# RWKV's block inverses: both chunks of a head in one product with the whole block-diagonal matrix

## The chip, the cores and the metric

The kernel runs on one core of one Trainium2 chip. Its time is the device time of one execution in microseconds (us). The core's engines are TensorE (PE in the profile, its loads of stationary operands PEld), VectorE (DVE), ScalarE (ACT), GpSimd (POOL) and SyncE (SP); each works through a queue of its own in order, and they meet at semaphores.

## The reference, cut to what matters

The program is three transformer layers over 512 tokens of 1024 features: an RWKV-7 time mix with a SwiGLU, a gated spatial mixer with a SwiGLU, and an attention layer with a feed-forward of 16384 single-neuron experts (PEER). All is float32. The change lies in the time mix, whose core is a recurrence over tokens, for each of 16 heads, with a 64x64 state S:

```
def step(S, inp):
    r_t, w_t, k_t, v_t, a_t, b_t = inp
    sa = jnp.einsum('bhij,bhj->bhi', S, a_t)
    S = (S * w_t[:, :, None, :] + sa[..., None] * b_t[:, :, None, :] + v_t[..., None] * k_t[:, :, None, :])
    y = jnp.einsum('bhij,bhj->bhi', S, r_t)
    return S, y
```

## The kernel before, in words

The recurrence is computed in chunks of 64 tokens. Inside a chunk the term `sa` of a token depends on those of the tokens before it, which makes a 64x64 unit triangular system for each head and chunk; its inverse, transposed, is the tile TT. A unit is 128 tokens (two chunks) by 8 heads, so there are 4 x 2 = 8 units. The rows of a tile are the 128 tokens, chunk 0 in partitions 0 to 63 and chunk 1 in 64 to 127.

A loop in `rwkv` (L607 to L618) staggers three stages of different units. For each k it writes out: the chain of unit k-3 (`wkv_chain`, which carries the state on), the solve of unit k-2 (`wkv_solve`), the preparation of unit k (`wkv_prep`), and the output step of unit k-3 (`wkv_post`, vector work).

- `wkv_prep` transposes its inputs on PE (L663), multiplies them (L678), copies the diagonal blocks into Ma on ACT (L681) and writes the masked products M on DVE (L682). The blocks go through DRAM (dl) into the tile L in which one 16x16 block has one partition; DVE inverts these small blocks (L704 to L719), and they return through DRAM to two tiles Nd and NdT in which they stand on the diagonal of each 64x64 block.
- `wkv_solve` multiplies the rest of the system with Nd (L740) and copies the result into Yd on ACT (L741), one copy for each chunk. Yd is 128 x 8 heads x 128: of a head's 128x128 matrix the two 64x64 blocks on the diagonal are written and the other two were set to zero at the start (`wkv_init`). Three products with Yd follow (L749), each with an addition of NdT on DVE (L750); the addition's result is the moving operand of the next product, and the third gives TT.
- `wkv_chain` uses TT (L780) between lines that multiply with M and the state (L773, L775, L785, L794, L795).

The work of all three stages is queued on PE together. The order in each engine's queue is made when the program is built, not by the order of the lines alone, so pieces of L749 stand between lines of the other stages. After the stage the program goes on with the output projection; its weights are split into two parts on ACT and DVE (L102, L103), and some of these splits stand among the last units' work.

A matmul takes a stationary operand, loaded first, and a moving one. In a product of L749 the stationary operand is one chunk's 64 columns of Yd (128 rows by 64 columns), the moving one is 64 columns of the current iterate, and the result goes to the 64 partitions of that chunk. A float32 matmul shows in the profile as two passes.

Of the kernel before, what the change touches and what calls it, by code (L numbers as in the profile page):

```python
# [40 lines left out]
class Kern:  # L41
# [689 lines left out]
    def wkv_solve(self, p2, Yd, u):  # L731

        nc = self.nc
        mm = nc.tensor.matmul
        Nd, NdT = u["N"]
        bk = self.bank("s")
        for c in range(2):
            r = slice(64 * c, 64 * c + 64)
            for e in range(8):
                mm(bk[r, e * 64:(e + 1) * 64], u["M"][r, c, e, r], Nd[r, e, :], start=True, stop=True)  # L740
            nc.scalar.copy(Yd[r, :, r], bk[r].rearrange("p (e n) -> p e n", e=8))  # L741
        cur = NdT
        for it in range(3):
            nxt = p2.tile([128, 8, 64], F32, name="TT" if it == 2 else "TTt", bufs=2)
            bk = self.bank("s")
            for e in range(8):
                for c in range(2):
                    r = slice(64 * c, 64 * c + 64)
                    mm(bk[r, e * 64:(e + 1) * 64], Yd[:, e, r], cur[:, e, :], start=True, stop=True)  # L749
            nc.vector.tensor_add(nxt, bk.rearrange("p (e n) -> p e n", e=8), NdT)  # L750
            cur = nxt
        u["TT"] = cur
# [929 lines left out]
```

## Time and profile before

| | |
|---|---|
| median of 3 runs | 3100.21 us (3096.3 to 3103.62) |
| the profiled execution | 3095.69 us, its span 3093.9 us |
| PE busy | 2951.7 us, 95% of the span, 16121 passes |
| PEld busy | 2483.1 us, 80% |
| DVE, ACT, POOL busy | 68%, 37%, 21% |
| granted clock of PE over the span | 0.971 of full speed |
| L749 in the trace | 768 passes between 333 and 490 us |

Busy shares are averages over stages of different kinds. Matmuls are pipelined, the next starts long before the last has ended, and the ends are modelled: the duration of a group is the time from its first start to its last end, and the distance between starts is what a pass costs its successors.

### The profile page before, as it was taken

The numbers are of one execution on the slowest core, as the hardware profiler recorded it, in microseconds if no ns is written. First come the engines' busy times: TensorE is split into PE (matmuls) and PEld (weight loads), VectorE is DVE, ScalarE is ACT, GpSimd is POOL, SyncE is SP. The second block draws the span as 40 slices with busy tenths as digits, with TensorE's granted clock in tenths as the row PEclk, the third lists the DMA queues.
The fourth block names the chain that finished last, engine by engine and source line by source line (L and its number), as shares of the span: only waits on it lengthen the run. The fifth ranks groups of instructions, "written<-read, shape, count | busy, mean of one in ns | idle before, by whom it ended". The sixth has DMA issues, their size and how long they took to land.

```text
span 3093.9 us, 43610 instructions
## 1 busy us (share of the span) xinstructions
PE 2951.7 (95%) x16121; PEld 2483.1 (80%) x16121; DVE 2091.1 (68%) x4694; ACT 1156.3 (37%) x1918; POOL 646.3 (21%) x593
## 2 busy tenths in 40 slices
PE   7977899999999999999999999989999999999998
PEld 6755787888888788888875888989999888787887
DVE  7663775533247666425776678999988477888787
ACT  5533433322223332223565433344433333333332
POOL 1023221000000000000000003345444434444453
PEclk9978999999999999999998999999999999999999
DMA  4235654222324267533220234678888889999996
GB/s 143 92 85 192 162 144 130 93 91 95 95 89 143 76 214 234 164 95 92 77 85 2 68 101 161 227 244 294 282 292 287 294 307 322 336 341 321 327 335 223
DMA packets 217553, 569.03 MB, mean 184 GB/s; under 512 B 64474, under 2 KB 80090, under 8 KB 217212
## 3 DMA queue, kind: packets, MB, share of 16 engines
q1 hardware_dynamic: 144508, 362.71, 35.8%
q0 software_dynamic: 64096, 200.89, 19.1%
q10 hardware_dynamic: 8736, 2.65, 0.4%
q8 instruction: 126, 2.06, 0.3%
q14 instruction: 87, 0.71, 0.1%
HBM read 504.24 MB, written 61.87 MB: 183 GB/s over the span
## 4 chain that ended last, share of the span: by engine, by line
PE 75%; DVE 12%; DMA 6%; issue 4%; ACT 2%; POOL 1%; POOLq 0%; SPq 0%; DVEq 0%; ACTq 0%
PE b L276 19%; PE b L124 15%; PE b L123 15%; PE b L122 15%; PE b L1470 3%; DMA gl<-ga 2%; DVE wlo L103 2%; DVE er L1304 1%; PE b L1161 1%; PE b L959 1%; DVE hr L1308 1%; DMA er<-in_pe_ur,eu 1%; PE b L1179 1%; DVE wk L1339 1%; PE b L678 1%
## 5 line engine op out<-in xcount | busy, mean ns | idle before, releaser
L102 ACT CAST whi<-wst 128x1024 fp32r<-128x1024 f32 (+2 forms) x491 | 510.7, 1041 | 1165.4 <-PE b L123 436.1
L103 DVE TENSOR_TENSOR wlo<-wst,whi 128x1024 fp32r<-128x1024 f32 (+2 forms) x466 | 563.3, 1210 | 442.5 <-ACT whi L102 426.2
L124 PE MATMUL b<-hTh,wlo 128*128 128x384 f32 (+2 forms) x1992 | 716.4, 360 | 13.7 <-DVE wlo L103 13.4
L122 PE MATMUL b<-hTh,whi 128*128 128x384 f32 (+2 forms) x1992 | 722.4, 363 | 2.5 <-ACT hTh L223 1.5
L123 PE MATMUL b<-hTl,whi 128*128 128x384 f32 (+2 forms) x1992 | 717.0, 360 | 2.2 <-DVE hTl L224 2.2
L124 PEld LDWEIGHTS b<-hTh,wlo 128*128 128x128 f32 x1992 | 377.7, 190 | 57.0 <-DVE wlo L103 18.4
L122 PEld LDWEIGHTS b<-hTh,whi 128*128 128x128 f32 x1992 | 379.2, 191 | 42.3 <-ACT hTh L223 2.2
L123 PEld LDWEIGHTS b<-hTl,whi 128*128 128x128 f32 x1992 | 378.4, 190 | 40.9 <-DVE hTl L224 3.0
L122 PE MATMUL b<-whi,ch 128*128 128x512 f32 x768 | 304.7, 397 | 5.4 <-ACT ch L102 5.4
L124 PE MATMUL b<-whi,cl 128*128 128x512 f32 x768 | 304.6, 397 | 1.2 <-DVE cl L103 1.2
L123 PE MATMUL b<-wlo,ch 128*128 128x512 f32 x768 | 304.5, 396 | 0.3 <-DVE wlo L103 0.3
L1292 POOL DMA_INDIRECT er<-in_pe_v,ev x128 | 196.0, 1531 | 241.1 <-DVE hr L1308 216.1
L1292 POOL DMA_INDIRECT er<-in_pe_ur,eu x128 | 171.6, 1340 | 90.1 <-DVE er L1304 58.5
L122 PEld LDWEIGHTS b<-whi,ch 128*128 128x128 f32 x768 | 144.8, 189 | 39.8 <-ACT ch L102 5.7
L124 PEld LDWEIGHTS b<-whi,cl 128*128 128x128 f32 x768 | 144.6, 188 | 36.8 <-DVE cl L103 2.0
L123 PEld LDWEIGHTS b<-wlo,ch 128*128 128x128 f32 x768 | 144.8, 189 | 34.9 <-DVE wlo L103 0.7
L1308 DVE SCALAR_TENSOR_TENSOR hr<-er,a,hr 128x1024 f32<-128x1024 f32 x127 | 164.4, 1294 | 0.1
L1304 DVE SCALAR_TENSOR_TENSOR er<-er,hr 128x1024 f32<-128x1024 f32 x128 | 156.3, 1225 | 8.5 <-DMA er<-in_pe_ur,eu 8.5
L1274 POOL DMA_DIRECT2D ga<-gl x112 | 64.8, 579 | 345.1 <-ACT gl L1269 332.0
L276 PE MATMUL b<-whi,hTh 128*128 128x512 f32 (+2 forms) x336 | 129.3, 386 | 0.8 <-ACT P L971 0.8
L276 PE MATMUL b<-whi,hTl 128*128 128x512 f32 (+2 forms) x336 | 129.4, 385 | 0.4 <-DVE hTl L103 0.4
L276 PE MATMUL b<-wlo,hTh 128*128 128x512 f32 (+2 forms) x336 | 129.6, 386 | 0.0
(556 smaller groups left out, 4954.8 us busy)
## 6 DMA issues: line engine op xcount, KB each, us to landing
wst<-in_pe_u SPq DMA_DIRECT2D x128, 512.0 KB, 4.7
wst<-in_pe_v SPq DMA_DIRECT2D x128, 512.0 KB, 6.2
wst<-in_ffn_gu SPq DMA_DIRECT2D x88, 512.0 KB, 3.7
wst<-in_ad_w SPq DMA_DIRECT2D x48, 512.0 KB, 4.1
wst<-in_ffn_dn SPq DMA_DIRECT2D x44, 512.0 KB, 3.6
ga<-gl POOLq DMA_DIRECT2D x112, 192.0 KB, 4.2
gl<-ga SPq DMA_DIRECT2D x112, 192.0 KB, 5.0
gd<-G SPq DMA_DIRECT2D x40, 512.0 KB, 6.5
```

The lines of the kernel that those rows point to most:

```text
L102: self.nc.scalar.copy(hi, src)
L103: (eng or self.nc.vector).tensor_sub(lo, src, hi)
L122: mm(out, a[0], b[0], start=start, stop=False)
L123: mm(out, a[0], b[1], start=False, stop=False)
L124: mm(out, a[1], b[0], start=False, stop=stop)
L276: self.nc.tensor.matmul(banks[t][:, :n], self.chunk(aT, a, k + kk)[:, t * 128:(t + 1) * 128], w[b][:, kk, :], start=seen[t] == 1, stop=see ...
L678: mm(bk[:, q * 256:(q + 1) * 256], BT[:, c, 2 * g + q, :], AT[:, c, 2 * g + q].rearrange("p e n -> p (e n)"), start=True, stop=True)
L1274: nc.gpsimd.dma_start(ga[j], act(j))
L1292: d = nc.gpsimd.indirect_dma_start(out=r, out_offset=None, in_=src, in_offset=bass.IndirectOffsetOnAxis(ap=idx[:, k:k + 1], axis=0))
L1304: d = nc.vector.scalar_tensor_tensor(r, r, 1.0, hr, op0=OP.mult, op1=OP.mult, accum_out=a0[:, k:k + 1])
L1308: d = nc.vector.scalar_tensor_tensor(y0, r, a0[:, k - 128:k - 127], y0, op0=OP.mult, op1=OP.add)
L1470: mm(bk[:, e * 128:(e + 1) * 128], oi[:, u % OT // 4, :, e], oj[:, w, u % OT // 4, :, e], start=(w == 0), stop=(w == 1))
```

## The change

The loop over the two chunks inside a product goes away. For each head the stationary operand is now all 128 columns of Yd, both diagonal blocks with the zeros beside them, and one matmul writes all 128 partitions of the result. The numbers that it computes are the same.

```
             bk = self.bank("s")
             for e in range(8):
-                for c in range(2):
-                    r = slice(64 * c, 64 * c + 64)
-                    mm(bk[r, e * 64:(e + 1) * 64], Yd[:, e, r], cur[:, e, :], start=True, stop=True)
+                mm(bk[:, e * 64:(e + 1) * 64], Yd[:, e, :], cur[:, e, :], start=True, stop=True)
             nc.vector.tensor_add(nxt, bk.rearrange("p (e n) -> p e n", e=8), NdT)
             cur = nxt
```

## Rows read from the trace of the kernel before

**Rows 1.** The page's part 4: the chain that ended last, share by engine.

```profile
PE 75%; DVE 12%; DMA 6%; issue 4%; ACT 2%; POOL 1%; POOLq 0%; SPq 0%; DVEq 0%; ACTq 0%
```

**Rows 2.** The chain of waits, 320 to 505 us: its lines, then pieces (start, us, what).

```profile
by line: PE b L749 9.2%; PE b L678 7.9%; PE b L780 7.9%; PE b L740 7.8%; PE b L795 6.7%; PE b L773 6.1%; PE b L775 5.9%; PE b L794 5.7%; DMA L<-dl 4.7%; DMA Nd<-Nd 4.4%; PE b L785 4.3%; DMA Nd<-N 4.3%; issue 3.5%; DMA dl<-Ma 2.4%; PE b L663
...
395.31 4.42 DMA dl<-Ma
...
421.21 4.66 DMA Nd<-Nd
```

**Rows 3.** Busy time by stretch: us, PE, PEld, DVE, ACT, POOL, clock, DMA share, GB/s.

```profile
329.00:342.70 13.70, 10.59 (x154) 8.57 (x155) 12.27 (x32) 5.54 (x11) 2.48 (x4) 1.00 0.81 179
342.70:394.20 51.50, 51.48 (x891) 46.30 (x891) 38.64 (x107) 18.38 (x34) 11.88 (x17) 1.00 0.61 151
394.20:403.90 9.70, 8.87 (x153) 7.95 (x152) 6.89 (x15) 2.53 (x5) 1.78 (x3) 1.00 0.54 143
403.90:420.30 16.40, 16.40 (x237) 14.63 (x237) 13.63 (x40) 7.08 (x14) 5.29 (x6) 1.00 0.52 146
420.30:425.90 5.60, 3.98 (x63) 3.44 (x61) 4.26 (x12) 3.91 (x7) 1.39 (x2) 1.00 0.83 199
425.90:443.00 17.10, 17.08 (x254) 15.76 (x255) 9.23 (x32) 4.70 (x9) 1.60 (x3) 0.90 0.71 187
443.00:452.70 9.70, 7.47 (x134) 6.67 (x133) 9.25 (x21) 2.52 (x5) 2.60 (x3) 1.00 0.40 79
...
463.00:480.00 17.00, 14.46 (x233) 13.37 (x231) 9.64 (x25) 4.18 (x7) 2.98 (x5) 0.80 0.50 125
```

**Rows 4.** The same view of L749 alone: us, PE (passes), PEld, clock, DMA, GB/s.

```profile
342.70:394.20 51.50, 11.50 (x256) 9.64 (x256) 1.00 0.61 151
...
425.90:443.00 17.10, 2.85 (x64) 2.35 (x64) 0.90 0.71 187
...
463.00:490.50 27.50, 8.75 (x192) 7.51 (x192) 0.88 0.41 110
```

**Rows 5.** Timeline, PE, 440 to 449 us: start, us, engine, line, operation, count.

```profile
440.76 1.15 PE L749 MATMUL b<-TTt,Y 128*64 128x64 f32 x32
...
441.84 0.48 PE L678 MATMUL b<-AT,BT 128*128 128x256 f32 x1
...
447.45 1.15 PE L780 MATMUL b<-Z,TT 128*64 128x64 f32 x16 [0.55 <-ACT Z L777]
```

**Rows 6.** Instructions of L749: ns min/median/max, first and last start, forms.

```profile
L749 PEld LDWEIGHTS b<-TTt,Y x512: 132/138/227, 337.0 to 489.2; 128*64 128x64 f32 x171
...
L749 PE MATMUL b<-Nd,Y x256: 222/222/270, 333.8 to 484.5; 128*64 128x64 f32 x128
```

**Rows 7.** Instructions of L872, a 128x128 stationary operand with 128 moving columns.

```profile
L872 PEld LDWEIGHTS b<-ws,vr x64: 188/192/192, 1026.1 to 1033.3; 128*128 128x128 f32 x64
...
L872 PE MATMUL b<-ws,vr x64: 272/275/275, 1026.4 to 1033.4; 128*128 128x128 f32 x64
```

**Rows 8.** Timeline, PE, around 153 and 1028 us: 128x128 stationary operands.

```profile
152.96 1.05 PE L551 MATMUL b<-ch,sg 128*128 128x2 f32 x8
...
1027.81 2.40 PE L872 MATMUL b<-ws,vr 128*128 128x128 f32 x20
```

**Rows 9.** Timeline, PE, 463 to 475 us: products of the seventh unit.

```profile
464.44 1.15 PE L749 MATMUL b<-Nd,Y 128*64 128x64 f32 x30 [0.41 <-ACT Y L741]
...
466.37 1.15 PE L749 MATMUL b<-TTt,Y 128*64 128x64 f32 x32 [0.78 <-DVE TTt L750]
...
468.78 1.95 PE L749 MATMUL b<-TTt,Y 128*64 128x64 f32 x32 [1.25 <-DVE TTt L750]
```

**Rows 10.** Timeline, DVE, 465 to 486 us.

```profile
468.04 0.68 DVE L750 TENSOR_TENSOR TTt<-b,Nd 128x512 f32<-128x512 f32 x1
...
484.36 1.22 DVE L103 TENSOR_TENSOR wlo<-wst,whi 128x1024 fp32r<-128x1024 f32 x1 [6.48 <-issue]
...
485.50 0.68 DVE L750 TENSOR_TENSOR TTt<-b,Nd 128x512 f32<-128x512 f32 x1
```

## The prediction

> **What bounds the kernel now.** I read the chain of waits first, for the whole program, to see which engine ends last: the matmuls of TensorE (PE) hold 75% of it [rows 1]. So PE time counts unless some other wait covers it, but that is an average over many stages, and the change touches one, the RWKV block inverses at L749, which run between 329 and 490 us. Next the chain of that stage alone: L749 is its largest single line, 9.2% of a window of 185 us, about 17 us [rows 2]. The reader is to compare this with all the time that L749 takes there. Then the stage in stretches, each engine's busy time beside its length [rows 3]: in 342.7 to 394.2, 403.9 to 420.3 and 425.9 to 443 PE is busy 51.48 of 51.50, 16.40 of 16.40 and 17.08 of 17.10 us. There every nanosecond added to a PE instruction moves all that follows. In the other stretches PE has idle time, and what ends it has to be asked one by one. Last, how many L749 passes lie in each [rows 4]. A product is a group of 32 passes today (8 heads, 2 chunks, and each fp32 matmul goes through PE as two passes, as the count of 768 for 8 units of 3 products shows [rows 6]). The full stretches hold 256, 64 and 64 passes (the first and the last of the three are shown): 12 of the 24 products.
>
> **What one product costs today.** The timeline shows one as 32 passes in 1.15 us [rows 5]. A pass lasts 0.22 us from its start to its modelled end [rows 6], so the starts spread over 0.93 us. The useful comparison is L780, which has the same 128x64 stationary tile and 64 moving columns but sends all of its 16 passes to one half of the output rows: it takes 1.15 us as well [rows 5]. So one pass alone holds its half of the array for 0.93/16 = 0.058 us, and in L749, whose passes alternate between the halves, two run side by side in that time. What the change proposes to save, half of the instructions, is already overlapped: 16 pairs at 0.058 us.
>
> **What one product costs after.** 16 passes, each with a 128x128 fp32 stationary tile and 64 moving columns. No instruction of this kernel has that shape. What sets its spacing is either the moving side, or the load of the stationary tile. The nearest row below on the moving side is L551: 128x128 fp32 stationary and only 2 moving columns, 8 passes in 1.05 us [rows 8]. With two columns to move, this can only be the load, and the spacing is at most 1.05/8 = 0.131 us, and 0.112 us if the last pass lasts about 0.27 us, as L872's do. The nearest row above is L872, 128x128 with 128 moving columns: 20 passes in 2.40 us, less the 0.275 us of the last, over 19 steps: 0.112 us [rows 7, 8]. Both sides give the same, so with 64 columns between them I take 0.112 us. One load lasts 0.192 us there against 0.138 us for 64 columns [rows 6, 7], which fits: twice the columns, 0.054 us more. The bounds are 0.058 us (a full-width load is as fast as a half one) and 0.131 us. One product then takes 16 x 0.112 = 1.79 us of PE instead of 0.93: 0.86 us more, between 0 and 1.17.
>
> **Which of the 24 lie on the path.**
> - The 12 of the full stretches: 12 x 0.86 = 10.3 us. PE never waits there, so nothing covers them.
> - The three of the first unit (before 342.7): PE is idle for 3.1 of 13.7 us [rows 3], ended mostly by vector work of other units and by a DMA that doesn't wait for L749. That takes most of 2.6 us; I charge 0.4 (bounds 0 and 2.6).
> - One in 394.2 to 403.9, where the chain runs through the round trip of the Ma blocks through DRAM (it starts with 4.42 us, dl<-Ma [rows 2]); one in 420.3 to 425.9, behind 4.66 us of Nd<-Nd [rows 2]; one in 443 to 452.7, where VectorE (DVE) is busy 9.25 of 9.70 us and PE 7.47 [rows 3]. PE catches up by the end of each wait: 0, and 0.86 each if that cover were gone.
> - The six of the last two units (463 to 490.5, 192 passes [rows 4]) run one after another, product, vector addition, product, with no other work to fill PE. The addition waits for the product, so latency counts. In the first of them PE starts at 464.44 and the addition follows at once: 0.9 with the longer first load. The second ends at 466.37+1.15 = 467.52, but its addition starts at 468.04, because DVE has a weight split (L103, 1.22 us a piece) and another step ahead of it [rows 9, 10]: 0.86-0.52 = 0.3. The third: 0.86. In the last unit the first product's last pass starts at 484.5 [rows 6] and ends 0.22 later, while DVE is in L103 until 485.5 [rows 10]: 0.1; the others 0.86 each. Together 3.9 us. A third product of 1.95 us there [rows 9] ran while the granted clock averaged 0.80 over its stretch [rows 3], partly at 1.2 GHz, the lower of the two levels; if such a time meets the longer product, it costs another 0.8, and as much comes back if the full clock is granted there.
>
> **Edges of a product.** When PE goes from a 64-column tile to a 128-column one, the next start comes later: the last L749 pass starts at 441.91-0.22 = 441.69 and L678 at 441.84, 0.15 us instead of 0.058 [rows 5], so 0.09 us for a change of shape. After the change L749 has the shape of L663 and L678, and these edges vanish, while new ones arise against the lines of the chain (L773 to L795), which keep 64 columns. In the three full stretches I count in the timeline 17 edges of the first kind and about 22 of the second, and the last two units a few more of the second: +0.7 us. The Trainium skill, "TensorEngine Tiling (Array Packing)", Key Properties, says that a change of the tiling mode, other than of the tile, drains the engine. By that an edge would cost 0.22-0.058 = 0.16 us and the same balance 1.2 us; the trace's 0.15 us between starts is less than a pass lasts, so the row decides.
>
> **What else the change touches.** The first pass of a product reads one chunk's columns of Yd today and both after, so it waits for both copies at L741. Some of today's products have their first two passes early for that reason; where the order puts the whole product straight behind, PE waits 0.41 us [rows 9], at most once a unit, 3.3 us in all; the rest of such a product stands behind that copy already, so I take 0. DVE's addition reads the same bank and only starts when the last pass is done. No DMA is issued, moved or removed. The order of PE's queue is made when the program is built, from estimates of durations that no trace shows; it cuts L749 into pieces between lines of other units. With half as many instructions it may move them: at worst the six products that I have outside the path in the first four stretches not called full come onto it (6 x 0.86 less the 0.4 charged, +4.8), at best their neighbours' idle time takes in more (-4.7, all of PE's idle time in the stretches at 394, 420 and 443 [rows 3]).
>
> **Sum.** 10.3 + 0.4 + 0 + 3.9 + 0.7 = 15.3 us. The profiled execution took 3095.69 us (span 3093.9 and 1.8 around it) and would take 3111.0. The runs shown have a median of 3100.21, 4.5 us more than this one execution, so against runs like them: 3115.5 us.
>
> **The rivals.**
> - *Half the instructions, half the time.* If 0.029 us per instruction were what issuing costs, and not two halves at 0.058, 16 passes would take 0.47 us, 0.46 less. Taken over 17 products (what the 14.6 us on the path come to at 0.86 each), it gives -7.8: 3092.4. It decides as soon as a full-width pass takes under 0.058 us. Against it stand L780, where a lone pass takes 0.058, and L551 with its 0.112. Chance 0.03.
> - *A full-width load is no longer than a half.* 16 x 0.058 is what the pairs take now: no change but the edges, 3100.9. For it: the array does load two halves at once in L749. Against it: L551, whose time nothing but a load of 128 columns can explain. Chance 0.08. The Trainium skill, "TensorE: Matmul & The Clock Gate", Weight-path perf modes, has a fast load for full 128-column weights that would do this, but excludes fp32, which is what these are.
> - *The idle time absorbs it.* The waits at 394, 420 and 443 take in delays of the full stretches ahead of them, 4.7 us, and the build's order puts half of the rest beside other work: about +5, 3105. For it: these waits end on DMA and DVE. Against it: their DMAs start only when PE's products are copied out (dl<-Ma after L678), so they move with PE. Chance 0.12.
> - *Edges and pieces cost more.* If PE lets a pass end before it takes another shape, an edge costs 0.22-0.058 = 0.16 us [rows 5, 6]. Over the whole stage I read about 54 edges against 64-column lines that arise if the product stays cut in as many pieces, and 24 against 128-column lines that go: 30 x 0.16 = +4.8 in place of 0.7, 3119.6; with the long spacing of 0.131 as well (17 x 1.17 = 19.9) 3125. For it: the pieces are there today. Against it: the edge of 0.15 us at 441.84. The rule on draining named above would be this case. Chance 0.12.
>
> **How the numbers follow.** The forecast has 0.65, with its own range of 3110 to 3120. It is the likeliest, so 3115.5. For 8 in 10 the range must hold it and the dearer rival and some of the absorbed case: 3104 to 3124; left out are the two cheap rivals (0.11) and the tails. About 0.2%, 6.2 us, is what a measurement of this kernel can tell from no change. Slower by more than that, over 3106.4: the forecast, the dearer rival and a third of the absorbed case, 0.81. Within: 0.15. Faster: 0.04.
>
> **What would show it.** In the changed kernel's profile L749 should have 384 passes instead of 768, 128x128 by 64, loads of 0.19 us, and a product of 16 passes should take about 1.9 to 2.0 us in the timeline (16 steps of 0.112 and a tail). The same stretch from 342.7 on should still be full of PE and end 7 us later; the pass from L749 to L678 should show no extra. The prediction is wrong if a product still takes 1.15 us (second rival) or less (first), or if products take 1.9 us and the end of the stage moves by under 6 us (third).

## The result, and the profile after

The changed kernel takes 3124.12 us against 3099.77 (medians of 4 runs each): 1.0081 of before, 95% interval 1.0060 to 1.0101, so 24.4 us more (18.6 to 31.3). Run twice again it was 1.0066 (1.0041 to 1.0090) and 1.0074 (1.0046 to 1.0102) of before. The forecast was 15.3 us more, 3115.5; its range ended at 3124. The way was right, the size was not.

First the chains again, as in [rows 1] for the program and [rows 2] for the stage, here from 320 to 525 us of the changed kernel (L747 and L748 are the lines that were L749 and L750):

```profile
PE 71%; DVE 13%; DMA 7%; issue 5%; ACT 2%; POOL 1%; POOLq 0%; DVEq 0%; ACTq 0%; SPq 0%
```

```profile
by line: PE b L747 21.5%; PE b L778 9.3%; PE b L678 8.5%; PE b L740 8.5%; PE b L771 7.4%; PE b L793 7.1%; PE b L773 6.6%; PE b L792 6.2%; PE b L783 4.7%; PE b L663 4.3%; issue 2.2%; DMA Nd<-N 2.0%; ACT wlo L779 1.4%; DMA Nd<-Nd 1.4%; DVE wl
```

The products hold 21.5% of 205 us, 44 us, where they held 17. Next the instructions of L747, against [rows 6, 7]: as many loads of 128 columns as expected (256 of this form, 128 of the other), and 0.192 us each. But some loads last up to 0.338 us and some matmuls up to 0.476, which the rows of before do not have to that extent.

```profile
L747 PEld LDWEIGHTS b<-TTt,Y x256: 186/192/338, 340.0 to 507.3; 128*128 128x128 f32 x128
L747 PE MATMUL b<-TTt,Y x256: 219/275/476, 340.2 to 507.4; 128*128 128x64 f32 x128
```

The timeline of PE shows which: products of the first six units, as the one at 453.18, take 2.00 us where they took 1.15 [rows 5], products of the last two up to 3.68.

```profile
452.97 0.28 PE L773 MATMUL b<-S,AT 128*64 128x64 f32 x2
453.18 2.00 PE L747 MATMUL b<-TTt,Y 128*128 128x64 f32 x16
455.01 1.08 PE L678 MATMUL b<-AT,BT 128*128 128x256 f32 x4
...
456.28 2.00 PE L747 MATMUL b<-TTt,Y 128*128 128x64 f32 x16
458.21 0.33 PE L773 MATMUL b<-S,AT 128*64 128x64 f32 x2
...
500.32 2.55 PE L747 MATMUL b<-TTt,Y 128*128 128x64 f32 x16 [0.79 <-DVE TTt L748]
...
504.16 3.68 PE L747 MATMUL b<-TTt,Y 128*128 128x64 f32 x16 [1.30 <-DVE TTt L748]
```

So I cut the stage (first transpose at L663 to the first transpose of the output projection at L216) where the sixth unit's TT is added, into its first six units and its last two. Busy time by stretch, columns as in [rows 3]; the last but two is the granted clock. The changed kernel:

```profile
288.20:458.30 170.10, 153.00 (x1663) 136.75 (x1664) 106.12 (x288) 64.13 (x125) 46.44 (x64) 0.95 0.61 162
458.30:521.60 63.30, 54.73 (x674) 51.80 (x674) 38.24 (x96) 16.30 (x25) 11.81 (x11) 0.81 0.34 95
```

The kernel before, in its first profile:

```profile
286.60:445.70 159.10, 138.46 (x1937) 120.02 (x1938) 105.44 (x285) 63.97 (x125) 45.55 (x63) 0.96 0.65 172
445.70:502.50 56.80, 46.53 (x788) 43.46 (x786) 37.80 (x102) 16.52 (x25) 9.06 (x10) 0.91 0.42 111
```

The first six units are 11.0 us longer at about the same clock (0.95 and 0.96). The last two are 6.5 us longer at a lower one. In these traces the clock is either full or at half (1.2 GHz), so a mean of 0.81 over 63.3 us means 24 us at half clock (0.19/0.5 of the time), against 10 before. The rest of the program has the same instructions in the same order. Its part with the second PEER tables, from the first product with ch to the last, was 614 us in that profile of before and 622 to 630 in nearly all later profiles of either kernel, so the 31 us between the two profiled spans hold some 10 us that do not belong to the change; the medians do not rest on them.

### The profile page after: what moved, and what is told of

Same layout as the page of the kernel before. It is cut to its first block, busy times and chain, and to the rows that moved or that the text cites. A ratio compares the mean times of both kernels' runs of the same rounds, so it can differ in the third digit from the quotient of the medians.

```text
span 3125.3 us, 42848 instructions
## 1 busy us (share of the span) xinstructions
PE 2977.0 (95%) x15737; PEld 2508.9 (80%) x15737; DVE 2095.5 (67%) x4694; ACT 1156.3 (37%) x1918; POOL 634.4 (20%) x593
## 4 chain that ended last, share of the span: by engine, by line
PE 71%; DVE 13%; DMA 7%; issue 5%; ACT 2%; POOL 1%; POOLq 0%; DVEq 0%; ACTq 0%; SPq 0%
PE b L276 18%; PE b L124 13%; PE b L123 13%; PE b L122 13%; DMA gl<-ga 3%; DVE wlo L103 3%; PE b L1468 3%; PE b L747 1%; DVE hr L1306 1%; DMA wst<-in_pe_v 1%; PE b L1159 1%; PE b L957 1%; DVE er L1302 1%; PE b L678 1%; DVE wk L1337 1%
## 5 line engine op out<-in xcount | busy, mean ns | idle before, releaser
L124 PEld LDWEIGHTS b<-hTh,wlo 128*128 128x128 f32 x1992 | 379.0, 190 | 62.5 <-DVE wlo L103 24.4
L1290 POOL DMA_INDIRECT er<-in_pe_v,ev x128 | 189.2, 1478 | 254.6 <-DVE hr L1306 228.2
```

What stands on the lines that cost most here:

```text
L124: mm(out, a[1], b[0], start=False, stop=stop)
L1290: d = nc.gpsimd.indirect_dma_start(out=r, out_offset=None, in_=src, in_offset=bass.IndirectOffsetOnAxis(ap=idx[:, k:k + 1], axis=0))
```

## The experiments

My theory at first was that the halves no longer run side by side, and that this is all; after the profile it had a second term, the clock in the last two units.

**The kernels again.** No edit.

> The kernel before once more, unchanged, for a second profile and the spread between executions. The stage with the block inverses (L663 to L795) should take the same 216 us to within 1 us. Theory 'the part behind 2470 us is as long as it happens to be' (it is full of transfers): its length of 614 us from the first matmul with ch there (2470.1) to the last (3084.4) differs between this profile and the first by several us. Theory 'the change makes the last part longer': it is 614 us again, within 1 or 2.

> The changed kernel once more, unchanged. Stage with the block inverses 17.6 us longer than in the kernel before, as in its first profile. Last part (628 us in the first profile of it): theory 'as it happens to be' 614 to 630, anywhere; theory 'the change makes it longer' 628 again, within 2. Time: 1.0081 of before, that is about +25 us, if the second holds; nearer to +18 if the first does.

> The changed kernel a third time, on the chip of the other two. Both theories: +18 to +23 against before. Theory of the fallen clock: 20 us or more of half clock in the last two units, rest of the stage 61 to 65 us. Rival 'luck': anything from 0 to 27.

The two stretches of before in its second profile:

```profile
289.10:445.60 156.50, 137.63 (x1934) 119.11 (x1935) 103.56 (x284) 63.83 (x125) 45.49 (x63) 0.95 0.66 175
445.60:498.60 53.00, 42.50 (x790) 39.56 (x788) 37.58 (x102) 16.41 (x25) 9.05 (x10) 1.00 0.45 119
```

Those of the changed kernel in its second profile, then in its third:

```profile
286.10:455.40 169.30, 154.09 (x1665) 136.69 (x1666) 105.60 (x289) 64.21 (x125) 46.04 (x64) 0.95 0.61 163
455.40:520.40 65.00, 56.48 (x675) 53.52 (x674) 37.79 (x96) 16.30 (x25) 12.17 (x11) 0.79 0.33 90
```

```profile
457.50:521.00 63.50, 54.96 (x675) 52.00 (x675) 36.96 (x96) 16.32 (x25) 12.21 (x11) 0.81 0.32 91
```

Before, the stage was 209.5 us this time and 215.9 the first, so not the same to within 1 us, and the clock of the last two units is what moved most: no half clock, then 10 us. After, the stage is the same three times (233.4, 234.3, 233.9), with 24 to 27 us of half clock each time. In means the first six go from 157.8 to 170.0, +12.2, and the last two from 54.9 to 63.9, +9.0: 21.2 us, which the three ratios (+25, +20, +23 us) hold. The last part was 624.5 us in both second profiles, so "as it happens to be" stands.

**The loops of a product exchanged.** Narrow passes, but neighbours in the same half:

```diff
-            for e in range(8):
-                for c in range(2):
-                    r = slice(64 * c, 64 * c + 64)
+            for c in range(2):
+                r = slice(64 * c, 64 * c + 64)
+                for e in range(8):
                     mm(bk[r, e * 64:(e + 1) * 64], Yd[:, e, r], cur[:, e, :], start=True, stop=True)
```

> The kernel before with the two loops of a product exchanged: all 8 heads of chunk 0, then all 8 of chunk 1. The same 32 passes of 64 columns, but neighbours go to the same half of the output. Theory 'what the change loses is the two halves side by side': a product takes 32 x 0.058 = 1.87 us of PE, as after the change (16 x 0.112 = 1.79), and the stage is 15 to 20 us longer than before, though no stationary operand is wider. Rival 'full-width loads are dear in themselves': a product stays at 0.93 to 1.0 us between its first and last start and the time stays within 3 us of before.

One of its products, and its two stretches:

```profile
471.15 1.90 PE L749 MATMUL b<-TTt,Y 128*64 128x64 f32 x32 [0.78 <-DVE TTt L750]
```

```profile
287.50:449.00 161.50, 145.89 (x1915) 128.90 (x1915) 104.02 (x281) 63.27 (x123) 45.62 (x63) 0.96 0.62 166
449.00:506.10 57.10, 47.96 (x807) 44.97 (x807) 39.42 (x104) 17.05 (x27) 9.17 (x10) 1.00 0.46 122
```

Two passes from its timeline, where a product is cut into pieces:

```profile
356.16 0.22 PE L773 MATMUL b<-wlo,M 128*64 128x64 f32 x1
356.16 0.22 PE L749 MATMUL b<-Nd,Y 128*64 128x64 f32 x1
```

A product takes 1.90 us, as the theory said: it is the pairing that made 1.15. But the time is only 1.0022 of before (1.0001 to 1.0044), +7 us, and the stage 6 us longer, not 15 to 20. Equal products, unequal path: PE is busy 146 us in the first six units here and 153 in the changed kernel. A narrow pass can run beside a neighbour of another line: the passes of L749 and L773 at 356.16 start within 10 ns of each other. The passes of a full-width product start 0.112 us apart at full clock. That this is the whole of the difference was not tested. There is no half clock in the last two units.

**Each full-width matmul cut in two of 32 columns.**

```diff
-                mm(bk[:, e * 64:(e + 1) * 64], Yd[:, e, :], cur[:, e, :], start=True, stop=True)
+                for z in range(2):
+                    mm(bk[:, e * 64 + 32 * z:e * 64 + 32 * z + 32], Yd[:, e, :], cur[:, e, 32 * z:32 * z + 32],
+                       start=True, stop=True)
```

> The changed kernel with each matmul cut in two of 32 moving columns: the full-width stationary operand is loaded twice as often, the columns moved stay the same. Theory 'the load of 128 columns sets the spacing': 0.11 us a pass whatever it moves, so 32 x 0.112 = 3.6 us a product, 1.8 more than after the change; over the 17 to 20 products that count, +30 to +37 us against the changed kernel, +48 to +60 against before. Rival 'the moving columns set it': a product stays at about 1.8 us, the time within 5 us of the changed kernel.

Two of its products on PE's timeline, then its first six units and its last two:

```profile
341.30 6.87 PE L748 MATMUL b<-TTt,Y 128*128 128x32 f32 x32
...
410.84 3.76 PE L748 MATMUL b<-TTt,Y 128*128 128x32 f32 x32
```

```profile
286.30:521.20 234.90, 218.06 (x1941) 198.09 (x1942) 104.15 (x288) 64.40 (x125) 47.28 (x66) 0.81 0.46 121
521.20:615.80 94.60, 83.79 (x781) 80.71 (x781) 37.76 (x97) 16.43 (x25) 9.16 (x9) 0.66 0.20 56
```

The load sets the spacing: 32 passes take 3.76 us at full clock, (3.76-0.28)/31 = 0.112 us each, with half the columns moved. The Trainium skill, "TensorE: Matmul & The Clock Gate", LDWEIGHTS, counts a load by the columns of the stationary operand alone, their number over 1.2 in ns, by which an estimate for 128 is 107 ns. The spacing in the traces agrees within 0.006 us, 0.112 us whether a pass moves 32, 64 or 128 columns, though the record of a single load lasts 0.192 us. But the time is 1.0356 of before (1.0322 to 1.0391), +110 us where 48 to 60 were expected. The product of 6.87 us shows the misfit: the clock was at 1.2 GHz for some 153 of the 329.5 us of this stage (0.19/0.5 of 234.9 and 0.34/0.5 of 94.6), while PE was busy 302 of them. At half speed that loses up to 77 us, against 8 to 12 for the 16 to 23 us of half clock in the stage before; it is enough for the 50 to 62 us that are missing. That made the clock the suspect for the last two units.

**Twice the columns for the same loads.** Seven of eight heads also move the next head's columns; the next matmul overwrites what that gives.

```diff
-                mm(bk[:, e * 64:(e + 1) * 64], Yd[:, e, :], cur[:, e, :], start=True, stop=True)
+                w = 2 if e < 7 else 1
+                mm(bk[:, e * 64:(e + w) * 64], Yd[:, e, :], cur[:, e:e + w, :].rearrange("p a b -> p (a b)"),
+                   start=True, stop=True)
```

> The changed kernel, but 7 of the 8 heads of a product move 128 columns instead of 64: their own and the next head's, whose result the next head's matmul then overwrites. More work for nothing, the load of 128 columns (0.112 us a pass) still hides it. In both profiles of the changed kernel the granted clock is at half for 27 and 24 us in the last two units, and products there take 3.5 instead of 2.0 us. Theory 'the clock falls because the passes load much and move little': with twice the columns moved it stays at full for most of it, products take 2.0, and from the end of the sixth unit's solve to the end of the stage it is 57 to 60 us instead of 63 to 65; the first six units are as in the changed kernel; 4 to 7 us less than it, +12 to +17 against before. Rival 'it falls because PE stands idle between product and addition': half clock and 64 us stay, +20.

> The kernel with 128 moving columns in every product once more, beside the changed kernel on the same chip, since how long the clock stays at half also differs between two profiles of one kernel (10 and 0 us in the last two units of the kernel before). Theory 'little moved per load lets the clock fall': little or no half clock in the last two units again, sixth solve at 170, rest 55 to 58; +7 to +13 against before, 8 to 13 less than the changed kernel of this call. Rival 'the first profile was luck': 10 to 27 us of half clock, +20, no difference to the changed kernel.

A product of the last unit and the two stretches in the first of these runs, then the last two units in the second:

```profile
500.18 2.00 PE L748 MATMUL b<-TTt,Y 128*128 128x128 f32 x16 [0.78 <-DVE TTt L750]
```

```profile
287.40:458.10 170.70, 151.54 (x1631) 134.47 (x1632) 113.05 (x291) 64.47 (x125) 48.33 (x64) 0.95 0.61 161
458.10:513.40 55.30, 49.08 (x706) 45.97 (x705) 35.70 (x94) 16.25 (x25) 11.15 (x11) 1.00 0.39 110
```

```profile
458.10:513.20 55.10, 49.11 (x706) 46.00 (x705) 35.64 (x94) 16.25 (x25) 11.50 (x11) 1.00 0.42 109
```

PE's wait of 0.78 us for the addition between two products is still there; the clock is not lowered, the product takes 2.00 us, and the last two units 55.3 and 55.1 us instead of 63.3 to 65.0. The first six are as in the changed kernel (170.7). The times are 1.0024 (1.0009 to 1.0038) and 1.0049 (1.0032 to 1.0066) of before, +7 and +15 us. More work, less time: the clock was worth 8 to 10 us there by the profiles. By the timed runs it is 13 us (1.0024 against 1.0066, taken apart) and 8 us (1.0049 against 1.0074, taken together, with intervals that overlap). These waits alone do not lower it.

**The same in the last two units only.** The edit above with `if late and e < 7`.

> The changed kernel with 128 moving columns in the last two units only. Theory: where PE is full the columns moved make no difference, so this is the same as moving 128 everywhere: sixth solve at 169 to 171, rest 55 to 58, +7 to +13. Rival 'it is all the extra columns before that hold the clock': half clock and 61 to 65 us in the last two units, +20.

```profile
462.70:520.90 58.20, 50.23 (x674) 47.35 (x674) 37.50 (x96) 16.30 (x25) 11.52 (x11) 0.94 0.37 102
```

Between the two: 7 us of half clock, 58.2 us, 1.0045 of before (1.0029 to 1.0061). The extra columns ahead are not needed for most of the effect. The first six took 175 us here, 4 of the 5 us above the changed kernel's in the first unit, where the code is the same. There the clock differs too; the same 20 us in this kernel and then in the first profile of the changed one:

```profile
330.00:350.00 20.00, 17.64 (x113) 16.32 (x114) 13.22 (x34) 5.75 (x11) 2.92 (x5) 0.74 0.76 177
```

```profile
330.00:350.00 20.00, 17.89 (x156) 16.26 (x155) 16.66 (x44) 7.45 (x16) 3.19 (x5) 0.91 0.79 187
```

This is 10 us at 1.2 GHz against 4 (0.26/0.5 and 0.09/0.5 of 20), and some 7 us more at half speed lose up to 3.5 of the 4 us. Why the clock was lower there in this profile is open.

**The change in part of the units.** `wkv_solve` is told whether its unit is among the first six, or the last two, and uses the changed matmul there.

> The change in the first six units alone, the last two as before. Theory (two terms: 0.86 us a product where PE is full, and a fallen clock in the last two units): the sixth solve ends 11 to 14 us later than before, counted from the stage's first transpose (170 us instead of 156 to 159), and the rest of the stage takes 53 to 57 us as before; +11 to +14. Rival 'one thing over the whole stage': each unit pays alike, so 6/8 of 20 us, +15, with half clock in the last two units here too.

> The change in the last two units alone. Theory of two terms: the sixth solve ends as before (156 to 159 us), the rest of the stage takes 62 to 65 us instead of 53 to 57, with products of 3.5 us at half clock; +6 to +10. Rival 'each unit pays alike': 2/8 of 20 us, +5, and no more half clock than before. My prediction's term without a change of the clock: +3.9.

Changed in the first six:

```profile
284.70:453.20 168.50, 153.87 (x1663) 136.47 (x1664) 106.04 (x288) 64.29 (x125) 46.40 (x64) 0.95 0.62 164
453.20:510.30 57.10, 45.44 (x770) 42.91 (x770) 37.10 (x96) 16.32 (x25) 12.69 (x11) 0.88 0.37 103
```

Changed in the last two, with two of its products:

```profile
286.30:441.40 155.10, 135.91 (x1925) 117.71 (x1926) 101.03 (x284) 63.97 (x125) 43.31 (x62) 0.97 0.67 176
441.40:504.60 63.20, 53.25 (x704) 50.12 (x702) 38.38 (x102) 16.43 (x25) 11.80 (x12) 0.89 0.39 102
```

```profile
463.55 2.42 PE L748 MATMUL b<-TTt,Y 128*128 128x64 f32 x16 [0.78 <-DVE TTt L753]
466.75 3.68 PE L748 MATMUL b<-TTt,Y 128*128 128x64 f32 x16 [0.78 <-DVE TTt L753]
```

The parts add up in time: 1.0042 (1.0026 to 1.0058), +13 us, for six units, 1.0034 (1.0017 to 1.0051), +11 us, for two. The lengths are within 1.5 us of where the theory of two terms has them: 168.5 and 57.1, 155.1 and 63.2. But the clock is not. With the change in the last two units alone these have 14 us of half clock (0.11/0.5 of 63.2), as many as with the change in the first six alone (0.12/0.5 of 57.1), where they are written as before; 14 us at half speed lose 7 at most. And the first part is 2.7 us shorter there than in the mean of before, so that this stage, 218.3 us, is 5.6 us longer than the mean of before and not 9 to 11. By the timed runs units do not pay alike, 2 us each in the first six and 5 in the last two; by this one profile the last two pay 3 each, and these two kernels do not show how much of it is the clock.

**L740 paired.** Its passes go one behind the other through one half, so the lesson read the other way is to pair them, in all units and then in the first six:

```diff
-        for c in range(2):
-            r = slice(64 * c, 64 * c + 64)
-            for e in range(8):
+        for e in range(8):
+            for c in range(2):
+                r = slice(64 * c, 64 * c + 64)
                 mm(bk[r, e * 64:(e + 1) * 64], u["M"][r, c, e, r], Nd[r, e, :], start=True, stop=True)
+        for c in range(2):
+            r = slice(64 * c, 64 * c + 64)
             nc.scalar.copy(Yd[r, :, r], bk[r].rearrange("p (e n) -> p e n", e=8))
```

> The kernel before with L740's loops exchanged: heads outside, chunks inside, and both copies to Yd after it. Its passes (64 rows by 64 columns) go one behind the other through one half today, 2 x 16 in 2 x 1.07 us. Theory 'neighbours in different halves run side by side': 32 passes start within about 1 us, 0.9 us less per unit of PE, 8 units, so -3 to -7 us against before (some of it hidden, and the first copy waits longer). Rival 'side by side only within 128 rows': L740 stays at 2 us a unit, no change.

> L740 paired (heads outside, chunks inside) in the first six units only; the last two as in the kernel before. With all eight paired the sixth solve ended at 154 us of the stage instead of 156.5 and 159.1, but the last two units had 20 us of half clock and the stage was no shorter (216.4 us). Theory 'the pairing gains, and the fallen clock took it back': sixth solve at 153 to 155, rest 53 to 57, stage 207 to 212, -2 to -5 us against before. Rival 'pairing L740 gains nothing on the path': stage 210 to 216, no difference.

All units paired, its L740 and its stretches; then the last two units with only the first six paired:

```profile
474.43 1.15 PE L740 MATMUL b<-Nd,M 64*64 64x64 f32 x32
```

```profile
286.60:440.70 154.10, 133.81 (x1940) 114.65 (x1941) 108.73 (x288) 63.83 (x125) 46.69 (x64) 0.94 0.65 174
440.70:503.00 62.30, 45.65 (x784) 42.82 (x782) 39.18 (x97) 16.30 (x25) 11.62 (x11) 0.84 0.42 111
```

```profile
442.30:503.30 61.00, 48.24 (x785) 45.24 (x783) 38.62 (x98) 16.43 (x25) 10.54 (x11) 0.86 0.45 114
```

Tiles of 64 rows run side by side too, 32 passes in 1.15 us instead of twice that, and the first six units gain 3 to 4 us. The last two give it back, with 20 and 17 us of half clock: 1.0020 (1.0002 to 1.0039) and 0.9997 (0.9975 to 1.0020) of before. In the second kernel these two units are written as before, so the expectation of 53 to 57 us failed, and what else sets the clock there stays open. No version beat the kernel before.

## Why the prediction was right and wrong

- *PE is the bound, and the pairs already overlap.* Right: exchanging the loops alone takes a product from 1.15 to 1.90 us, and the products' share of the stage's chain grew from 9.2 to 21.5%.
- *16 passes at 0.112 us instead of 16 pairs at 0.058.* Right at full clock: 2.00 us a product, with the load as what sets it.
- *Twelve products in full stretches, 10.3 us, three at the start 0.4, three covered.* Together with the edges 11 us for the first six units; measured +12.2 in means, and +13 in time with the change there alone. The edges behave as said. L678 follows the last pass of L747, which starts at 455.18-0.275 = 454.91, by 0.10 us, so this edge is gone. The new ones cost 0.09 us each: L747 at 453.18 follows the last pass of L773, which starts at 452.97+0.28-0.22 = 453.03, by 0.15 us instead of 0.058, and L773 at 458.21 follows the last pass of L747 (456.28+2.00-0.275 = 458.005) by 0.205 us instead of 0.112. In the first six units the trace has 32 of the new edges, against 24 of the old kind before: 8 x 0.09 = +0.7, as charged.
- *The six products of the last two units, "Together 3.9 us".* This is the step that failed. They cost 9.0 us in means of the profiles, and 11 (5 to 16) in time with the change there alone, though 5.6 by that kernel's one profile. With the clock at full they cost 2.2 us (55.2 with 128 columns moved, against 53.0 before), less than charged; the other 6.8 us are put down to the clock by subtraction. I had written that a product at 1.2 GHz "costs another 0.8, and as much comes back", once, from the one product of 1.95 us in [rows 9], and put it at nothing in the sum. In the changed kernel the time at 1.2 GHz was 24 to 27 us in three profiles, against 0 and 10 in two of before, and then everything in that time is slower, the chain's passes too, not the product alone. Where the last two units run at full clock on both sides, the stage is 226.0 and 225.8 us (128 columns moved) against 209.5 before, 16.5 and 16.3 us longer, close to the sum of 15.3; the timed runs of that kernel, +7 and +15 us, agree once of two. What lowers the clock stays open: it was at half for 14 us with the change in these two units alone, and for up to 20 us in kernels that leave these products as they were.
- *The rivals.* None was the case: the edges did not cost more, the idle time took in no more than I had charged it with. The case that came was missing from the list.

## What to carry to other kernels

Before joining two matmuls that fill half of the array each, look whether their starts come in pairs: if so they already run side by side, and the joined one pays a load of twice the columns. Count what a change does to the granted clock as a term of the sum of its own, by what the profile shows of the stretch: here products wait for a vector step and the clock already fell now and then [rows 3, 9], and with twice the load for the same columns moved it fell in every profile, for 14 to 27 us of some 64. A stretch whose clock varies between profiles of one kernel needs several profiles before a few microseconds there mean anything.

## What the runs showed of the hardware that was not expected

PE's clock fell to 1.2 GHz for 89 of 234.9 us in a stretch in which PE was busy 93% of the time by the profile, when the full-width passes of its products moved 32 columns. With 64 columns it fell for 24 to 27 of some 64 us of the last two units, three times of three, and for 14 us with the change in those units alone. With 128, at the same spacing of the passes, it did not fall there, twice of two, and for 7 us with 128 in those units alone. Where it does or doesn't fall with narrow passes (0 to 20 us in the same two units over six profiles) these runs do not settle.
